# Four PSUM banks for transposes and four for products behind an out-projection

## The chip, the cores and the metric

The kernel runs on one core of a Trainium2 chip. The metric is the device time of one execution in microseconds, taken as the median of several runs; beside it there is one execution under the hardware profiler, whose page and trace are read here. TensorE is called PE (PEld for its weight loads), VectorE DVE, ScalarE ACT, GpSimdE POOL, and the queue that issues most loads SP.

## The reference

One layer of a hybrid encoder on 1024 tokens with 1024 channels, in float32:

```python
h = rms_norm(x, mix_pre_norm)
proj = h @ w_in                                   # 1024 x 2472
o_gdn = gated_deltanet_group(...)                 # chunkwise delta rule, 4 heads
o_mla = mla_group(...)                            # latent attention, 8 heads, block-causal
mixed = concatenate([o_gdn, o_mla], -1) @ w_out
x = x + rms_norm(mixed, mix_post_norm)
h = rms_norm(x, ffn_pre_norm)
f = square(relu(h @ w_up)) @ w_down               # 1024 -> 4096 -> 1024
x = x + rms_norm(f, ffn_post_norm)
```

Only the part from `w_out` to `w_up` bears on the change.

## The kernel before

Every float32 product is made of three passes in a reduced type: both operands are split into a high and a low half (`hi`, `lo`), and `mm3` (L206 to L209) multiplies hi x hi, lo x hi and hi x lo into one PSUM bank. ACT makes the high half by a cast, DVE the low half by a subtraction; both read the same source. One 128x512 product of three passes over four blocks of rows is thus 12 PE instructions.

The tokens are handled in eight blocks of 128 rows, t = 0 to 7. The end of the mixer and the start of the channel mixer go like this:

- `out_proj(t)` (L1236) adds the attention heads' part of the output projection to what is kept in `part[t]`, in two banks of tag `out` (for t from 2 on). It then normalises: the row sums of squares on ACT, a chain of small DVE instructions, and at L1256 the last reads of the two banks, by DVE. A residual addition and a second normalisation follow, and the result is written back to `part[t]`.
- `put(block, src, c)` (L1275) brings 128x512 of it to the layout that the next product needs: four PE transposes into one bank of tag `tr` (tile `ps_h2T`, L1279), then per pair of target tiles a cast by ACT (L1284) and a subtraction by DVE (L1285), which both read that bank. One such group is called a put here.
- `ffn_in(t)` (L1291) calls `put`. For blocks 0 to 3 it fills the tiles `B11` and `B21`. The up-projection works on 2x2 blocks with seven products in place of eight, for which blocks 4 to 7 are combined with blocks 0 to 3: for each of them five puts fill `T1`, `T2`, `T4`, `B22` and `T3`, with a DVE addition or subtraction of rows ahead of most. So there are 20 puts for blocks 4 to 7.
- `filler(p)` (L1357) does two of the products of every second weight pair ahead of time, since they need only `B11` and `B21`: 12 instructions against `B11` into a bank of tag `ps` (tile `ps_up`), a copy out of it by ACT (L1370) and to memory, 12 instructions against `B21` into the same bank, then relu and square by ACT (L1378, L1379) and a store (L1380). There are eight of them, 192 PE instructions. Their weights arrive by loads in the order of use (`load_chained`, L183), into buffers that become free when an earlier filler has been stored or when a row tile has been transposed.
- `up_pair(p)` (L1427) then does the rest of the up-projection pair by pair, beginning with `T1` times the pair's weight sums. `prepare(p)` (L1405) makes these sums (L1413, L1414) and splits them (L1336, L1337).

The text calls the fillers the first to the eighth, and the halves of one its B11 and its B21 half. The instructions are recorded by a tile layer that sets semaphores, hands out buffers and orders the instructions of each engine by a model of its own, so that the order in which an engine runs them is not the order of the lines. Each engine and the load queue run their own order strictly in sequence.

PSUM has eight banks of 128x512 float32 values. `psum_pool` gives them out by tag: it ends the pool before and opens a new one, in which each tag has so many banks, taken in turn; a tile in a new pool waits for the tiles that lay in its bank before.

```python
    def psum_pool(name, **bufs):                                   # L122
        ps_stack.close()
        pp[:] = [ps_stack.enter_context(tc.tile_pool(name=name, bufs=1, space=PSUM, reuse_waits="tile")), bufs]
...
    psum_pool("psC", out=4, tr=2, ps=2)                            # L1214
...
        ps = psum("ps_h2T", "tr")                                  # L1277, in put
        for j in range(4):
            transpose(ps[:, j * P : (j + 1) * P], src[:, j * P : (j + 1) * P], ident)
        n = 4 // len(block)
        for i, pair in enumerate(block):
            hi, lo = cut(pair, slice(None), slice(None), slice(c * P, (c + 1) * P))
            s = blocks3(ps[:, i * n * P : (i + 1) * n * P])
            nc.scalar.copy(hi, s)
            nc.vector.tensor_sub(lo, s, hi.bitcast(F32))
```

The stage's outer loop (L1477 to L1497) runs `out_proj` for all blocks, with `ffn_in` for blocks 0 to 3 two blocks behind and one filler's steps at the end; then `ffn_in` for blocks 4 to 7 with a step of a filler at each of its yields; then the rest of the fillers and the first `prepare`; and last `psum_pool("psD", ps=8)` for the up-projection.

Of the kernel before, what the change touches and what calls it, by code (L numbers as in the profile page):

```python
# [104 lines left out]
def build(tc, a, out):  # L105
# [16 lines left out]
# [3 lines that stand above are left out]
        for tag in bufs:  # L125
            psum2("order") if tag == "ps2" else psum("order", tag)
# [3 lines left out]
    def psum(name, tag="ps"):  # L130
        return pp[0].tile([P, HALF], F32, name=name, tag=tag, bufs=pp[1][tag])

    def psum2(name):
        return pp[0].tile([P, 2, HALF], F32, name=name, tag="ps2", bufs=pp[1]["ps2"])
# [1101 lines left out]
    def out_proj(t):  # L1236
        h = part[t]
        xt = gtile("xt")
        nc.sync.dma_start(xt, a["x"][t * P : (t + 1) * P, :])
        if t not in early:  # L1240
            ss1[t] = small([2], "ss1")
            banks = [psum("ps_out", "out") for n in range(2)]
            for n, ps in enumerate(banks):

                other = h[:, n * HALF : (n + 1) * HALF]
                nc.scalar.copy(ps, other)
                out_pairs(ps, t, n, range(NPAIR), onto=True)
                nc.scalar.activation(other, ps, AF.Square, accum_out=ss1[t][:, n : n + 1])
        else:
            banks = [h[:, :HALF], h[:, HALF:]]  # L1250
        ss = ss1[t]
        nc.vector.tensor_scalar(ss[:, 0:1], ss[:, 0:1], ss[:, 1:2], None, op0=ALU.add)
        r = rstd_of(ss[:, 0:1], D, "rpost")
        for n, ps in enumerate(banks):
            s = slice(n * HALF, (n + 1) * HALF)
            nc.vector.scalar_tensor_tensor(h[:, s], ps, r, gb[:, s], op0=ALU.mult, op1=ALU.mult)  # L1256
        nc.vector.tensor_add(xt, xt, h)
        nc.scalar.dma_start(d_x1[t], xt)
        ss2 = small([1], "ss2")
        nc.scalar.activation(h, xt, AF.Square, accum_out=ss2)  # L1260
        r2 = rstd_of(ss2, D, "rffn")
        nc.vector.scalar_tensor_tensor(h, xt, r2, gf, op0=ALU.mult, op1=ALU.mult)
# [28 lines left out]
    def ffn_in(t):  # L1291

        h = part[t]
        if t < 4:
            put(B11, h[:, first_half], t)
            put(B21, h[:, second_half], t)
            return
        if t == 4:
            later.update(T1=big("T1", bp, "b"), B22=big("B22", bp, "b"), T2=halves_of("T2", mtile))
        o, c = part[t - 4], t - 4  # L1300
        t2 = gtile("t2")[:, :HALF]
        nc.vector.tensor_sub(o[:, first_half], h[:, first_half], o[:, first_half])
        put(later["T1"], o[:, first_half], c)
        yield
        nc.vector.tensor_sub(t2, h[:, second_half], o[:, first_half])
        put(later["T2"], t2, c)
        yield
        nc.vector.tensor_sub(o[:, second_half], o[:, second_half], t2)
        if t == 4:
            later.update(T4=halves_of("T4", mtile), T3=halves_of("T3", gtile))  # L1310
        put(later["T4"], o[:, second_half], c)
        yield
        put(later["B22"], h[:, second_half], c)
        yield
        nc.vector.tensor_sub(h[:, first_half], h[:, second_half], h[:, first_half])
        put(later["T3"], h[:, first_half], c)
        part[t] = part[t - 4] = None
        yield
# [104 lines left out]
    def run(g):  # L1423
        if g is not None:
            next(g, None)
# [52 lines left out]
    for t in range(NT):  # L1478
        out_proj(t)
        if 2 <= t < 6:  # L1480
            for _ in ffn_in(t - 2):
                pass
        if t >= 6:
            run(fill)
            run(fill)
    for t in range(4, NT):
        for _ in ffn_in(t):
            run(fill)
# [237 lines left out]
```

## Time and profile before

| | |
|---|---|
| median of three runs | 1275.88 us (1275.73, 1275.88, 6953.69) |
| the profiled execution | 1274.2 us |
| its span, first to last instruction | 1272.5 us |
| TensorE busy | 1223.9 us, 96% of the span |
| VectorE, ScalarE, GpSimdE busy | 901.6, 656.4, 160.0 us |
| mean granted TensorE clock | 0.988 of full speed |
| moved by DMA | 205.72 MB, 162 GB/s |

The profile's page gives these sums. The stage of the change lies at about 600 to 700 us of the span, the up-projection behind it. In rows of the timeline, a line number names the line of the kernel, the arrow goes from what is read to what is written, and brackets give the idle time of the engine before the instruction with what ended it. The views by stretches give the busy time of each engine, then the granted clock (1.00 is full speed), the share of DMA engines in use and GB/s.

### The profile page before, as it was taken

How to read it: one execution, taken by the hardware profiler on the slowest of the kernel's cores; microseconds unless marked ns; L12 is line 12 of the kernel's file. 1: busy time of each engine (PE TensorE's matmuls, PEld its weight loads, DVE VectorE, ACT ScalarE, POOL GpSimd, SP SyncE). 2: the span in 40 equal slices, each digit the busy share in tenths (PEclk: the TensorE clock that was granted, in tenths of full speed). 3: DMA queues.
4: the chain of work that ended last, by engine and by line, in shares of the span. 5: the costliest groups of instructions: out<-in, count | busy, mean ns of one | idle time of the engine just before them, and what ended most of it. 6: DMA issues, size and time to landing. Idle time of an engine off the chain costs nothing.

```text
span 1272.5 us, 17691 instructions
## 1 busy us (share of the span) xinstructions
PE 1223.9 (96%) x6228; PEld 1035.0 (81%) x6228; DVE 901.6 (71%) x1779; ACT 656.4 (52%) x1201; POOL 160.0 (13%) x148
## 2 busy tenths in 40 slices
PE   7999999999889999999898999999999999999997
PEld 6978888899778878887686888888888888888885
DVE  7678879645556786686985677768666687775665
ACT  6467743325645786675665445445445443343341
POOL 1011001220044553430000000000000000010120
PEclk9999999999999999999998999999999999999998
DMA  5124534736342511123454355454449984547821
GB/s 234 34 75 146 190 120 174 232 79 182 97 145 87 162 50 31 42 67 150 148 186 161 124 181 210 165 198 174 174 157 388 400 323 153 193 159 237 282 89 66
DMA packets 111219, 205.72 MB, mean 162 GB/s; under 512 B 33558, under 2 KB 51990, under 8 KB 111131
## 3 DMA queue, kind: packets, MB, share of 16 engines
q1 hardware_dynamic: 93696, 171.90, 40.3%
q10 hardware_dynamic: 17434, 32.70, 6.9%
q8 instruction: 49, 0.80, 0.3%
q14 instruction: 40, 0.32, 0.1%
HBM read 143.07 MB, written 61.49 MB: 161 GB/s over the span
## 4 chain that ended last, share of the span: by engine, by line
PE 63%; DVE 3%; ACT 3%; DMA 2%; issue 1%; POOL 0%; SPq 0%; ACTq 0%; DVEq 0%; POOLq 0%
PE ps_up L208 8%; PE ps_up L209 8%; PE ps_up L207 8%; PE ps_dn L208 8%; PE ps_dn L209 8%; PE ps_dn L207 8%; PE ps_PT L1061 2%; PE ps_out L207 2%; PE ps_out L209 2%; PE ps_out L208 2%; PE ps_o L1080 1%; PE ps_sc L207 1%; PE ps_o L1079 1%; PE ps_sc L208 1%; PE ps_sc L209 1%
## 5 line engine op out<-in xcount | busy, mean ns | idle before, releaser
L1588 POOL TENSOR_TENSOR rows<-rows,gpost 128x512 f32<-128x512 f32 x12 | 20.1, 1703 | 617.8 <-ACT junk L1585 617.8
L209 PE MATMUL ps_proj<-hThi,wlo 128*128 128x512 f32 x192 | 75.1, 395 | 1.2 <-DVE wlo L199 1.2
L207 PE MATMUL ps_proj<-hThi,whi 128*128 128x512 f32 x192 | 76.0, 396 | 0.0
L208 PE MATMUL ps_proj<-hTlo,whi 128*128 128x512 f32 x192 | 76.0, 396 | 0.0
L1065 DVE TENSOR_TENSOR PTlo<-ps_PT,PThi 128x512 fp32r<-128x512 f32 (+2 forms) x96 | 52.0, 550 | 20.0 <-ACT PThi L1064 19.3
L1064 ACT CAST PThi<-ps_PT 128x512 fp32r<-128x512 f32 (+2 forms) x96 | 45.3, 480 | 30.1 <-PE ps_PT L1061 28.5
L1520 DVE TENSOR_TENSOR dlo<-draw,dhi 128x1024 fp32r<-128x1024 f32 x35 | 44.7, 1293 | 21.6 <-ACT dhi L1519 21.5
L208 PE MATMUL ps_dn<-dlo,dhi 128*128 128x512 f32 x144 | 56.0, 389 | 0.0
L209 PE MATMUL ps_dn<-dhi,dlo 128*128 128x512 f32 x144 | 56.0, 389 | 0.0
L1519 ACT CAST dhi<-draw 128x1024 fp32r<-128x1024 f32 x35 | 36.2, 1050 | 37.9 <-issue 13.8
L207 PE MATMUL ps_dn<-dhi 128*128 128x512 f32 x144 | 55.0, 389 | 0.0
L1035 ACT ACTIVATE Pt<-ps_sc,nm 128x896 f32<-128x896 f32 (+3 forms) x64 | 47.9, 749 | 11.8 <-DVE nm L1033 7.6
L1336 ACT CAST whi<-raw 128x1024 fp32r<-128x1024 f32 (+1 forms) x29 | 25.9, 904 | 51.4 <-PE ps_up L208 49.7
L1061 PE MATMUL ps_PT<-ident,Pt 128*128 128x128 f32 x288 | 46.4, 275 | 3.2 <-DVE PTlo L1065 1.9
L1033 DVE TENSOR_REDUCE nm<-ps_sc 128x1 f32<-128x896 f32 (+3 forms) x64 | 47.8, 750 | 1.2
L199 DVE TENSOR_TENSOR wlo<-raw,whi 128x1024 fp32r<-128x1024 f32 (+1 forms) x27 | 33.8, 1254 | 18.1 <-ACT whi L198 15.5
L1040 POOL TENSOR_TENSOR Pt<-Pt,rs 128x128 f32<-128x128 f32 (+4 forms) x40 | 35.4, 884 | 88.5 <-DVE rs L1038 64.4
L209 PEld LDWEIGHTS ps_proj<-hThi,wlo 128*128 128x128 f32 x192 | 36.1, 188 | 9.2 <-DVE wlo L199 1.7
L1079 PE MATMUL ps_o<-PThi,V 128*128 128x256 f32 (+1 forms) x160 | 40.5, 276 | 2.9 <-DVE o L1086 1.2
L208 PEld LDWEIGHTS ps_proj<-hTlo,whi 128*128 128x128 f32 x192 | 36.1, 188 | 7.4 <-issue 0.5
L207 PEld LDWEIGHTS ps_proj<-hThi,whi 128*128 128x128 f32 x192 | 36.1, 188 | 7.4 <-issue 0.5
L1061 PEld LDWEIGHTS ps_PT<-ident,Pt 128*128 128x128 f32 x288 | 34.0, 140 | 8.6 <-issue 2.5
(596 smaller groups left out, 3978.0 us busy)
## 6 DMA issues: line engine op xcount, KB each, us to landing
draw<-in_w_down_dram SPq DMA_DIRECT2D x47, 512.0 KB
draw<-d_act SPq DMA_DIRECT2D x41, 512.0 KB
raw<-in_w_up_dram SPq DMA_DIRECT2D x40, 512.0 KB
raw<-in_w_down_dram SPq DMA_DIRECT2D x17, 512.0 KB
raw<-in_w_qkvg_dram SPq DMA_DIRECT2D x16, 512.0 KB
d_act<-c SPq DMA_DIRECT2D x16, 512.0 KB
d_act<-s SPq DMA_DIRECT2D x16, 512.0 KB
raw<-d_act SPq DMA_DIRECT2D x15, 512.0 KB
```

Of the source, the lines that this page charges most:

```text
L207: mm(ps, lhs[0], rhs[0], start=start, stop=False, **kw)
L208: mm(ps, lhs[0], rhs[1], start=False, stop=False, **kw)
L209: mm(ps, lhs[1], rhs[0], start=False, stop=stop, **kw)
L1033: nc.vector.tensor_reduce(nm, ps[:, :npc, :w], axis=AX.XY, op=ALU.max, negate=True)
L1035: nc.scalar.activation(Pt[:, :n].rearrange("p (i w) -> p i w", i=npc), ps[:, :npc, :w], AF.Exp, bias=nm, scale=1.0, accum_out=sm)
L1040: nc.gpsimd.tensor_tensor(Pt[:, :n], Pt[:, :n], rs.to_broadcast([P, n]), op=ALU.mult)
L1061: transpose(ps[:, j * P : (j + 1) * P], Pt[:, b * P : (b + 1) * P], ident)
L1064: nc.scalar.copy(hi[:, :n, cs], ps3)
L1065: nc.vector.tensor_sub(lo[:, :n, cs], ps3, hi[:, :n, cs].bitcast(F32))
L1079: mm(ps[:, cs], V[h][:, b], hi[:, cs], start=(b == 0), stop=False)
L1519: nc.scalar.copy(hi, raw)
L1520: nc.vector.tensor_tensor(lo, raw, hi.bitcast(F32), op=ALU.subtract)
```

## The change

One line is added, ahead of the loop over blocks 4 to 7:

```diff
         if t >= 6:
             run(fill)
             run(fill)
+    psum_pool("psT", tr=4, ps=4)
     for t in range(4, NT):
         for _ in ffn_in(t):
             run(fill)
```

Until now the pool of L1214 held for the whole stage: four banks for `out_proj`, two for puts, two for products. Now its eight banks are given out anew once the last `out_proj` has been recorded: four for puts, which lie where the four of `out` were, and four for products, which lie where `tr` and `ps` were. Since the first filler is recorded before this line, it still uses a bank of the old pool, and all 20 puts of blocks 4 to 7 and the other seven fillers use the new one. As the banks enter into what the tile layer orders, the order of the instructions changes on PE, DVE and ACT from here to the first product with `T1`. Up to here and, but for buffer numbers and a few single rows, from there on it is as it was.

On PE, the first filler ends its B11 half like this in the order before (`part_4795` is the row tile of block 0, here being put into T1 with block 4 subtracted):

```order
L207 MATMUL ps_up<-B11hi,whi 128x512
L208 MATMUL ps_up<-B11lo,whi 128x512
L209 MATMUL ps_up<-B11hi,wlo 128x512
L1279 MATMUL ps_h2T<-ident,part_4795 128x128 x4
L208 MATMUL ps_up<-B11lo,whi 128x512
L209 MATMUL ps_up<-B11hi,wlo 128x512
L207 MATMUL ps_up<-B11hi,whi 128x512
```

And like this in the order of the change:

```order
L207 MATMUL ps_up<-B11hi,whi 128x512
L208 MATMUL ps_up<-B11lo,whi 128x512
L209 MATMUL ps_up<-B11hi,wlo 128x512
L207 MATMUL ps_up<-B21hi,whi 128x512
L208 MATMUL ps_up<-B21lo,whi 128x512
L209 MATMUL ps_up<-B21hi,wlo 128x512
L207 MATMUL ps_up<-B21hi,whi 128x512
```

Block 4's first put and the second filler's B11 half stood between the two halves of the first filler; now the B21 half follows directly, and that put comes after its twelve instructions.

On PE, the last puts stand like this in the order before, at the end of the eighth filler (`part_5806` and `part_5975` are the rows of blocks 6 and 7, `part_5308` those of block 3, `t_7272` a difference of both):

```order
L1279 MATMUL ps_h2T<-ident,part_5806 128x128 x4
L208 MATMUL ps_up<-B21lo,first_hi 128x512
L209 MATMUL ps_up<-B21hi,first_lo 128x512
L1279 MATMUL ps_h2T<-ident,part_5806 128x128 x4
L1279 MATMUL ps_h2T<-ident,part_5308 128x128 x4
L1279 MATMUL ps_h2T<-ident,t_7272 128x128 x4
L1279 MATMUL ps_h2T<-ident,part_5308 128x128 x4
L1279 MATMUL ps_h2T<-ident,part_5975 128x128 x8
L207 MATMUL ps_up<-T1hi,wv_hi 128x512
```

And like this in the order of the change, in the B21 half of the sixth filler:

```order
L1279 MATMUL ps_h2T<-ident,t_7278 128x128 x4
L1279 MATMUL ps_h2T<-ident,part_5308 128x128 x4
L207 MATMUL ps_up<-B21hi,whi 128x512
L208 MATMUL ps_up<-B21lo,whi 128x512
L1279 MATMUL ps_h2T<-ident,part_5975 128x128 x4
L209 MATMUL ps_up<-B21hi,wlo 128x512
L207 MATMUL ps_up<-B21hi,whi 128x512
L208 MATMUL ps_up<-B21lo,whi 128x512
L209 MATMUL ps_up<-B21hi,wlo 128x512
L1279 MATMUL ps_h2T<-ident,part_5975 128x128 x4
L207 MATMUL ps_up<-B21hi,whi 128x512
```

The six puts at the end stood behind all fillers, with two products ahead of the last five; now products stand between them, and from the last put to the first product with `T1` there are 49 products of fillers.

On ACT, the casts of weights stand like this in the order before, in the middle of the fillers (`whi<-raw_7300` and `first_hi<-raw` are the seventh and eighth filler's weights, and the casts from `ps_h2T` belong to the puts of blocks 4 and 5):

```order
L1336 CAST whi<-raw_7153 128x1024
L1371 DMA d_p_102<-raw 128x512
L1336 CAST whi<-raw 128x1024
L1284 CAST T3hi_7036<-ps_h2T 128x2x128
L1284 CAST T1hi<-ps_h2T 128x4x128
L1378 ACTIVATE raw<-ps_up 128x512
L1379 ACTIVATE raw<-raw 128x512
L1284 CAST T3hi_7038<-ps_h2T 128x2x128
L1380 DMA d_act_109<-raw 128x512
L1336 CAST whi<-raw_7300 128x1024
L1378 ACTIVATE raw<-ps_up 128x512
L1336 CAST first_hi<-raw 128x1024
```

And like this in the order of the change (`raw_7306` is the seventh filler's weights there, `d_act_108` the store of the second filler):

```order
L1336 CAST whi<-raw_7306 128x1024
L1379 ACTIVATE raw<-raw 128x512
L1371 DMA d_p_101<-raw 128x512
L1370 COPY raw<-ps_up 128x512
L1380 DMA d_act_108<-raw 128x512
L1371 DMA d_p_102<-raw 128x512
L1284 CAST T2hi_6993<-ps_h2T 128x2x128
L1284 CAST T2hi_6995<-ps_h2T 128x2x128
L1284 CAST T4hi_7038<-ps_h2T 128x2x128
L1284 CAST T4hi_7040<-ps_h2T 128x2x128
L1336 CAST first_hi<-raw 128x1024
```

The weights' casts have moved ahead in relation to the fillers' results: the seventh filler's cast now stands before the second filler's square and store, and the eighth filler's cast only one store and two puts behind.

## The prediction

> **What bounds the kernel now.** The page comes first: how much of the span is TensorE, and how it runs where nothing disturbs it.
>
> ```profile
> span 1272.5 us, 17691 instructions
> PE 1223.9 (96%) x6228; PEld 1035.0 (81%) x6228; DVE 901.6 (71%) x1779; ACT 656.4 (52%) x1201; POOL 160.0 (13%) x148
> 800.00:1000.00 200.00, 199.95 (x881) 165.01 (x880) 136.25 (x175) 92.03 (x114) 0.00 (x0) 1.00 0.62 228
> ```
>
> TensorE is busy for 96% of the span. The third row is a stretch of the view by stretches (length, then busy time and count of PE, PEld, DVE, ACT and POOL, granted clock, DMA share, GB/s): 200 us of the up-projection, 881 products of 512 columns without a gap, so **0.227 us per product**. A change of banks removes no work; it can only win TensorE's idle time and its time at a low clock. So the second view looks for both around the edited line, which stands between the out-projection and the last blocks' transposes.
>
> ```profile
> 684.00:688.00 4.00, 2.51 (x17) 1.70 (x16) 2.56 (x5) 3.17 (x7) 0.00 (x0) 1.00 0.41 158
> 688.00:692.00 4.00, 1.48 (x8) 0.87 (x6) 4.00 (x8) 3.40 (x7) 0.00 (x0) 0.63 0.39 131
> 692.00:696.00 4.00, 2.17 (x8) 1.91 (x9) 4.00 (x7) 1.82 (x4) 0.00 (x0) 0.50 0.60 195
> 696.00:700.00 4.00, 4.00 (x12) 3.19 (x11) 4.00 (x8) 1.65 (x3) 0.00 (x0) 0.59 0.19 72
> ```
>
> Here is the hole: 16 us with PE busy for 10.2, and the clock at 0.50 to 0.63 for most of it. The timeline of PE alone says what it waits for (start, length, instruction, idle time before it and its releaser).
>
> ```profile
> 684.36 0.60 PE L1279 MATMUL ps_h2T<-ident,part 128*128 128x128 f32 x4
> 685.46 0.66 PE L1279 MATMUL ps_h2T<-ident,part 128*128 128x128 f32 x4 [0.50 <-DVE B22lo L1285]
> 686.91 0.63 PE L1279 MATMUL ps_h2T<-ident,t 128*128 128x128 f32 x4 [0.79 <-DVE T3lo L1285]
> 687.73 0.66 PE L1279 MATMUL ps_h2T<-ident,part 128*128 128x128 f32 x4 [0.20 <-DVE T1lo L1285]
> 690.62 1.09 PE L1279 MATMUL ps_h2T<-ident,part 128*128 128x128 f32 x4 [2.23 <-DVE T2lo L1285]
> 693.83 1.08 PE L1279 MATMUL ps_h2T<-ident,part 128*128 128x128 f32 x4 [2.12 <-DVE T4lo L1285]
> 694.56 0.78 PE L207 MATMUL ps_up<-T1hi,wv_hi 128*128 128x512 f32 x1
> ...
> 699.58 0.40 PE L207 MATMUL ps_up<-T2hi,wv_hi 128*128 128x512 f32 x1
> ```
>
> Six puts (four transposes each, into one bank) stand at the end with no products left between them. Each is released by the DVE subtraction that empties the bank of the put two before it: two banks, so each put waits for ACT's cast and DVE's subtraction. DVE is 4.00 of 4.00 busy from 688 on, since the first pair's weight sums stand in its queue between those subtractions. The first product runs at a halved clock, and full pace is back at 699.58.
>
> **The change, part by part.** First the price of a put, from the stretch before the hole, where puts stand between products:
>
> ```profile
> 637.81:684.13 46.32, 46.32 (x231) 38.37 (x230) 29.21 (x55) 25.86 (x53) 0.00 (x0) 1.00 0.55 192
> 637.81:684.13 46.32, 7.61 (x52) 6.40 (x53) 10.01 (x21) 8.68 (x22) 1.00 0.55 192
> ```
>
> The second row is the same stretch for ps_h2T alone: 52 transposes, 13 puts. Of the other 179 matmuls one began before it; (46.32 - 178 x 0.227) / 13 = 0.455 us per put.
>
> *The hole goes (-9.8).* From 684.36 to 699.58 are 15.2 us. Their work at full pace is 6 x 0.455 + 12 x 0.227 = 5.45 us, so 9.8 us are lost. In the changed order all puts stand among fillers, 49 filler products follow the last one, and a put waits for the fourth put before it. What must keep up is DVE:
>
> ```profile
> 636.00:700.00 64.00, 58.16 (x275) 47.37 (x275) 45.58 (x82) 36.65 (x72) 0.00 (x0) 0.91 0.49 173
> ```
>
> Its 45.6 us of this stretch must fit into 64 - 7.3 = 56.7 us: 80%, so the cover holds on average.
>
> *A wait for the out-projection's banks (0).* The new transposes' banks lie where `out` lay, so block 4's T1 and T2 wait for the last readers of out_proj(6)'s banks, T4 and B22 for those of out_proj(7)'s.
>
> ```profile
> 640.83 1.40 DVE L1256 SCALAR_TENSOR_TENSOR part<-ps_out,rpost,gpost 128x512 f32<-128x512 f32 x2
> ```
>
> These end at 642.23, and DVE's new order puts them ahead of T1lo, so no later. PE comes to T4 at 645.6 (below). The 3.4 us between are the cover; beyond it every us costs one, since all of PE's queue stands behind that put.
>
> *The first filler now stands alone (+0.5).* Before, T1's put and the second filler's products lay between its B11 and B21 halves. Now its B21 half follows at once, into the same bank, which ACT must copy first.
>
> ```profile
> 636.10 0.63 PE L209 MATMUL ps_up<-B11hi,wlo 128*128 128x512 f32 x1
> 636.53 1.05 PE L1279 MATMUL ps_h2T<-ident,part 128*128 128x128 f32 x4
> 637.24 0.74 PE L208 MATMUL ps_up<-B11lo,whi 128*128 128x512 f32 x1
> 637.81 0.40 PE L209 MATMUL ps_up<-B11hi,wlo 128*128 128x512 f32 x1
> 636.82 0.58 ACT L1370 COPY raw<-ps_up 128x512 f32<-128x512 f32 x1 [4.31 <-PE ps_up L209]
> ```
>
> The twelfth product starts at 636.10, the copy ends at 637.40, PE resumes at about 637.45. From 636.53 to 637.81 it does 0.84 of a product (0.36 / 0.427) instead of a put and a whole one: behind by 0.455 + 0.04 = 0.5 us. The queue behind this product holds everything.
>
> *The clock comes back later (+1.6).* These are stretches of 3.41 us between the edges of the granted clock:
>
> ```profile
> 627.57:630.98 3.41, 0.87 (x5) 0.33 (x3) 2.47 (x8) 2.75 (x6) 0.00 (x0) 1.00 0.08 32
> 630.98:634.39 3.41, 2.86 (x7) 2.15 (x7) 3.41 (x11) 0.99 (x2) 0.00 (x0) 0.50 0.00 0
> 634.39:637.81 3.42, 3.42 (x11) 2.73 (x10) 3.42 (x7) 0.77 (x2) 0.00 (x0) 0.50 0.00 0
> 637.81:641.22 3.41, 3.41 (x16) 2.82 (x15) 3.41 (x8) 2.14 (x4) 0.00 (x0) 1.00 0.58 231
> 695.83:699.25 3.42, 3.42 (x9) 2.65 (x9) 3.42 (x8) 1.42 (x2) 0.00 (x0) 0.50 0.25 96
> ```
>
> PE waits for B11 from 627.85 to 630.38, and from 630.98 the clock is 0.50. A stretch with 2.86 of 3.41 busy is followed by another at 0.50; full ones (634.39, 695.83) are followed by 1.00. With the new wait the stretch 634.39 to 637.81 holds 636.73 - 634.39 + 0.36 = 2.7 us, less than 2.86. So I take one more stretch at half pace: 3.41 x (1 - 0.227 / 0.427) = 1.6 us, with 0.427 the step from 636.10 to 636.53. The bounds are 0 and two stretches, 3.2; I take one, by the row of 2.86. The Trainium skill, "TensorE: Matmul & The Clock Gate", section "What's actually happening", says that the clock is judged in free-running windows of 3413 ns and released after one busy window. The trace agrees in the grid: from 630.98 to 637.81 are two windows, from there to 699.25 eighteen. By that rule with only a full window counting as busy the sum gets this 1.6, with a four-fifths one 0.
>
> *Loads and ACT's queue (+0.4).* The last fillers' weights are cast ahead of block 5's and 6's evacuations in ACT's new order, and DVE's subtraction `first_lo` stands ahead of those too. The load of the last filler's weights waits for the store of the second filler's result.
>
> ```profile
> 655.76 1.67 SPq L183 DMA_DIRECT2D raw<-in_w_up_dram  x1
> 661.93 1.06 ACT L1336 CAST first_hi<-raw 128x1024 fp32r<-128x1024 f32 x1 [1.05 <-DMA raw<-in_w_up_dram]
> 663.02 1.22 DVE L1337 TENSOR_TENSOR first_lo<-raw,first_hi 128x1024 fp32r<-128x1024 f32 x1
> 686.00 0.33 ACTq L1380 DMA_DIRECT2D d_act<-raw  x1
> 688.05 5.65 SPq L183 DMA_DIRECT2D raw<-in_w_up_dram  x3
> ```
>
> A load takes up to 6.2 us (655.76 to 661.93), a store frees its buffer after about 2 (686.00 to 688.05). By the cadence above (637.45, plus 0.227 a product, 0.455 a put, and 1.8 for the half clock since 637.45) PE comes to T4's put of block 4 at 645.6 (24 products, 2 puts), ends the second filler at 652.4 (46, 6), comes to block 6's T4 at 668.5 (105, 12) and to the first T1 product at 689.2 (180, 20). The second filler's square follows on ACT by 655 to 658, its store at 656.4 to 658.3, the load 2 us later, the data at 662.5 to 666.5, and after cast, `first_lo` and B22lo (1.06 + 1.22 + 0.7) block 5's bank is free at 665.5 to 669.5, where 668.5 is needed; the next bank is needed 0.45 later and comes 0.4 + 0.7 later. So 0 to 1.6 us; I take 0.4, as only the late end of each estimate misses.
>
> *The sum:* -9.8 + 0.5 + 1.6 + 0.4 = -7.3 us. The profiled execution took 1274.2 us, its span of 1272.5 and 1.7 around it: 1266.9. The median of the runs is 1275.88, 1.7 above that execution; on its scale 1268.6, which I give. All else in the built program keeps its order but for single rows, and the up-projection stays without gaps, as in 800 to 1000.
>
> **The rivals.**
>
> *The clock returns at 637.81 all the same.* For it: 2.7 busy is near 2.86, and another execution's grid lies elsewhere. Against: the row of 2.86. The sum is 1.6 better: 1267.
>
> *The first pair's weights become the wait.* Before, they were ready just ahead of their use:
>
> ```profile
> 677.74 1.09 SPq L183 DMA_DIRECT2D raw<-in_w_up_dram  x2
> 687.59 0.68 DVE L1413 TENSOR_TENSOR sums<-raw 128x512 f32<-128x512 f32 x1
> 690.99 1.22 DVE L1337 TENSOR_TENSOR wv_lo<-sums,wv_hi 128x1024 fp32r<-128x1024 f32 x1
> ```
>
> If `wv_lo` still ended at 692.2 (690.99 + 1.22), the third T1 product would wait for it from 689.7: 2.5 us, and by the row of 627.57 such an idle window can halve the clock again for one or two windows, 1.6 to 3.2. That gives 1271 to 1274.5. For it: its loads still wait for the fillers' stores and stand last in SP's queue. Against: they wait for the third and fourth filler's stores alone, and by the cadence those end at 661.5 and 665.6; with 4 us for ACT and the store the loads start 7 to 12 us before 677.74.
>
> *Slower than before: the last filler's load starves the banks.* One mechanism: PE's queue stands at block 6's puts behind ACT's cast of weights that have not landed. Each us after about 665.5 costs one, and 1.6 to 3.2 once a window is half idle; the gain of 7.3 is eaten from a landing at about 670.5 on, 8 us later than the early estimate. It would give 1276 to 1282. For it: ACT and DVE are strictly in order there. Against: the longest load in the rows above took 6.2 us, and the DMA share is 0.55.
>
> *It does not do what it says:* the puts move, but the waits move with them to other bank reuses inside the fillers, and DVE's total sets the pace after all: 1275 to 1277. Against: the 80% of DVE.
>
> **How the numbers follow.** Forecast 0.54 (1265.5 to 1271), clock back early 0.20 (1264 to 1268), weights 0.15, slower 0.07, nothing gained 0.04. A range from 1263.5 to 1274.5 leaves out the last two and some edge of the others, less than 2 in 10, and holds the bounds of the clock (0 to 3.2) and of the loads (0 to 1.6). A measurement of this kernel can tell about 2% from no change, 25.5 us. No case but a pile-up of several stalls or an unseen gain reaches that: faster 0.01, within 0.98, slower 0.01.
>
> **What would show it.** In the changed profile: no idle row at L1279 after the fillers, and T1's first product at about 689 with the clock at 1.00; a wait of about 0.9 us of L207 (ps_up from B21) for ACT's copy near 637; the clock at 0.50 until about 641; PE in 700 to 1000 as full as now. The forecast is wrong if L1279 waits for B22lo or T1lo near 668, if L209 on `wv_lo` waits at 689, or if the half clock comes again between 641 and 690.

## The result, and the profile after

The changed kernel took **1267.7 us** (median of six runs, 1266.31 to 1268.59), the kernel before 1275.89 in the same set (six runs from 1272.38 on; one of them, 6953.69, stands far outside and is left out of the comparison). The ratio is 0.9937, with a 95% interval of 0.9921 to 0.9952. The forecast was 1268.6 within 1263.5 to 1274.5. Run again beside the experiments, in another set, the ratio was 0.9959 (0.9939 to 0.9978), with 1268.13 against 1274.15.

The page of the changed kernel:

```profile
span 1265.9 us, 17687 instructions
PE 1220.9 (96%) x6228; PEld 1032.8 (82%) x6228; DVE 898.9 (71%) x1779; ACT 655.2 (52%) x1201; POOL 160.1 (13%) x148
```

The work is the same, the span is 6.6 us shorter. What PE waits for from 600 to 705 us (engine, line, releaser; then us in total, times, longest):

```profile
PE ps_up L207 <- ACT B11hi L1284: 2.6, 1, 2.6
PE ps_out L207 <- ACT ps_out L1246: 2.3, 3, 1.4
PE ps_up L207 <- ACT raw L1370: 2.0, 2, 1.3
PE ps_up L208 <- DVE B11lo L1285: 0.8, 1, 0.8
```

No wait of L1279 is left: the six puts that stood at the end of the fillers now run among them without idle time. Two waits for ACT's copy (L1370) are new. The timeline of PE has both, and the two ends of the stretch in which the change acts:

```profile
625.75 0.40 PE L209 MATMUL ps_out<-whi,mixlo 128*128 128x512 f32 x1
636.67 0.80 PE L207 MATMUL ps_up<-B21hi,whi 128*128 128x512 f32 x1 [0.73 <-ACT raw L1370]
...
680.32 0.39 PE L209 MATMUL ps_up<-B11hi,wlo 128*128 128x512 f32 x1
...
683.04 0.39 PE L209 MATMUL ps_up<-B11hi,first_lo 128*128 128x512 f32 x1
684.73 0.50 PE L207 MATMUL ps_up<-B21hi,whi 128*128 128x512 f32 x1 [1.30 <-ACT raw L1370]
690.31 0.39 PE L207 MATMUL ps_up<-T1hi,wv_hi 128*128 128x512 f32 x1
693.03 0.39 PE L207 MATMUL ps_up<-T2hi,wv_hi 128*128 128x512 f32 x1
```

**The stretch** is taken from the start of the out-projection's last product to the start of the first product with T2. Here it is 693.03 - 625.75 = 67.28 us. In the kernel before, that last product began at

```profile
626.57 0.40 PE L209 MATMUL ps_out<-whi,mixlo 128*128 128x512 f32 x1
```

and with T2 at 699.58 it was 73.01. So the stretch is 5.7 us shorter; behind it lie 572.9 us in both (1265.9 - 693.03 and 1272.5 - 699.58). The other 0.8 us of the two spans' difference come ahead of the change (625.75 against 626.57).

The granted clock around the first filler, in stretches between its edges (length, busy time of PE, PEld, DVE, ACT, POOL, then clock, DMA share, GB/s; such a stretch of 3.41 us is called a window from here on):

```profile
626.79:630.20 3.41, 0.73 (x4) 0.19 (x1) 2.43 (x8) 2.76 (x6) 0.00 (x0) 1.00 0.09 36
630.20:633.61 3.41, 2.72 (x6) 2.15 (x7) 3.41 (x11) 0.98 (x2) 0.00 (x0) 0.50 0.00 0
633.61:637.03 3.42, 2.69 (x7) 1.67 (x6) 3.42 (x7) 0.58 (x1) 0.00 (x0) 0.50 0.00 0
637.03:640.44 3.41, 3.41 (x9) 2.64 (x9) 3.41 (x7) 1.15 (x2) 0.00 (x0) 0.50 0.58 231
```

The half clock lasts three windows, where it lasted two: the new stall of 0.73 us falls into the second. The new stall at 684.73 is read from DVE's and ACT's timelines:

```profile
678.83 0.69 DVE L1413 TENSOR_TENSOR sums<-raw 128x512 f32<-128x512 f32 x1 [4.25 <-DMA raw<-in_w_up_dram]
679.43 0.42 DVE L1285 TENSOR_TENSOR T2lo<-ps_h2T,T2hi 128x256 fp32r<-128x256 f32 x1
679.88 0.37 ACT L1284 CAST T2hi<-ps_h2T 128x256 fp32r<-128x256 f32 x1 [4.01 <-DVE T2lo L1285]
684.07 0.61 ACT L1370 COPY raw<-ps_up 128x512 f32<-128x512 f32 x1
```

DVE stands idle for 4.25 us before the first pair's weight sum, whose load has not landed. Behind it waits a subtraction of a put, behind that ACT's next cast, and behind ACT's casts the copy of the seventh filler's B11 half, whose last product began at 680.32. PE does the eighth filler's B11 half meanwhile (to 683.04), then comes to the seventh's B21 half, which goes into the bank still to be copied, and waits.

### The profile page after: what moved, and what is told of

Its sections match the earlier page's. It is cut to its first block, busy times and chain, and to the rows that moved or that the text cites. A ratio compares the mean times of both kernels' runs of the same rounds, so it can differ in the third digit from the quotient of the medians.

```text
span 1265.9 us, 17687 instructions
## 1 busy us (share of the span) xinstructions
PE 1220.9 (96%) x6228; PEld 1032.8 (82%) x6228; DVE 898.9 (71%) x1779; ACT 655.2 (52%) x1201; POOL 160.1 (13%) x148
## 4 chain that ended last, share of the span: by engine, by line
PE 61%; ACT 4%; DVE 4%; DMA 2%; issue 1%; POOL 0%; ACTq 0%; SPq 0%; DVEq 0%; POOLq 0%
PE ps_dn L208 8%; PE ps_dn L209 8%; PE ps_dn L207 8%; PE ps_up L207 7%; PE ps_up L208 7%; PE ps_up L209 7%; PE ps_PT L1061 2%; PE ps_out L207 2%; PE ps_out L209 2%; PE ps_out L208 2%; PE ps_o L1080 1%; PE ps_sc L207 1%; PE ps_o L1079 1%; PE ps_sc L208 1%; PE ps_sc L209 1%
```

## The experiments

Whole runs of one kernel differ by 2 to 11 us within a set (the changed one: 1266.31 to 1268.59 in one set, 1265.6 to 1272.1 in another; the one before: 1269.77 to 1280.38), so each experiment has its ratio and beside it the stretch of its profiled execution, as defined above, with what lies behind it. The sets differ in level, so medians are compared within a set only:

| kernel | ratio to before (95%) | stretch, us | from T2's first product to the end, us |
|---|---|---|---|
| before | 1 | 73.01 | 572.9 |
| changed | 0.9937 (0.9921 to 0.9952) | 67.28 | 572.9 |
| changed, again | 0.9959 (0.9939 to 0.9978) | 66.69 | 573.2 |
| tr=2, ps=2 | 1.0065 (1.005 to 1.008) | 79.52 | 572.9 |
| tr=4, ps=2 | 0.9967 (0.9954 to 0.998) | 65.76 | 572.6 |
| tr=2, ps=4 | 1.0078 (1.006 to 1.0096) | 77.71 | 572.7 |
| tr=3, ps=5 | 1.0015 (1.0 to 1.0029) | 73.06 | 572.9 |
| two products in the first filler's stall | 0.9944 (0.9932 to 0.9956) | 64.66 | 572.7 |
| ten products ahead of the first filler | 0.9945 (0.9924 to 0.9965) | 64.19 | 572.6 |
| sums behind the last put | 0.9947 (0.9928 to 0.9966) | 65.44 | 572.6 |
| both of these | 0.9962 (0.9948 to 0.9976) | 63.36 | 572.8 |
| another ring of load buffers | 1.0006 (0.9989 to 1.0024) | 63.81 | 580.1 |
| two buffers exchanged | 0.9943 (0.9928 to 0.9958) | 65.58 | 572.5 |
| exchanged, and ten products | 0.9953 (0.9939 to 0.9968) | 62.44 | 573.5 |

The theory: the transposes' banks carry the gain, and it is smaller than the hole because of the clock's third window and two stalls at ACT's copy. The rivals: the new order alone carries it, or the products' banks do; and the half clock has nothing to do with the stall.

### Which banks carry the gain

```diff
-    psum_pool("psT", tr=4, ps=4)
+    psum_pool("psT", tr=2, ps=2)
```

> The pool is opened anew at the same line, but with two banks for transposes and two for products, as before the change; four banks stay unused. Theory (the number of transposes' banks carries the gain): the last six puts stand behind the fillers again and wait as before, so the hole of 9.8 us stays, and the first filler stands alone as in the changed kernel, so its stall (0.5) and the third window at half clock (1.6) are paid without the gain: 1276 to 1279, at or above the kernel before (1275.9). Rival (any second pool at this place, by the new order that it brings, gives the gain): 1267 to 1270.

```diff
-    psum_pool("psT", tr=4, ps=4)
+    psum_pool("psT", tr=4, ps=2)
```

> Only the transposes get banks: four for them, two for products. Theory: the whole gain is here, since a filler's product waits for the bank of two products back, which a square or a copy freed long ago: 1266.5 to 1269.5, within 1 us of the changed kernel (1267.7). Rival (the product banks carry it): 1275 to 1279, with PE waiting for the bank of the filler before.

```diff
-    psum_pool("psT", tr=4, ps=4)
+    psum_pool("psT", tr=2, ps=4)
```

> Only the products get banks: two for transposes, four for products. Theory: the six puts at the end wait for DVE's subtractions again: 1275 to 1279. Rival (product banks): 1267 to 1270.

Measured were 1280.0, 1267.97 and 1282.62 us beside 1272.15 of the kernel before in that set. So only the version with four banks for transposes is faster; with two it is slower than before, whether products have two banks or four. (With tr=2, ps=4 the stretch explains 4.7 of the 10.5 us; in its profiled execution the rest lies ahead of the stretch, and why is open.) The timeline of PE with tr=2, ps=2, at the end of the fillers, shows where most of the 7.9 us go that it loses, more than the 0 to 3 of the theory:

```profile
688.99 0.66 PE L1279 MATMUL ps_h2T<-ident,t 128*128 128x128 f32 x4 [1.81 <-DVE T1lo L1285]
692.73 1.09 PE L1279 MATMUL ps_h2T<-ident,part 128*128 128x128 f32 x4 [2.64 <-DVE T2lo L1285]
695.93 1.09 PE L1279 MATMUL ps_h2T<-ident,part 128*128 128x128 f32 x4 [2.12 <-DVE T4lo L1285]
700.73 0.76 PE L207 MATMUL ps_up<-T1hi,wv_hi 128*128 128x512 f32 x1 [3.72 <-DVE T3lo L1285]
```

These waits sum to 10.3 us, where the six puts and the first product with T1 waited for 0.50 + 0.79 + 0.20 + 2.23 + 2.12 = 5.8 before. With the stall of the first filler (its price in the forecast: 0.5) and the third window (1.6) that makes 4.5 + 2.1 = 6.6, and the stretch is 6.5 longer. So with two banks the puts wait as before (6.6 us against 5.8), and most of the loss is side costs of opening the pool anew.

The largest of these, the 3.72 us, is one that the theory had not. The product with T1 reads nothing of T3, so what it waits for must be its bank: in the up-projection's pool it lies where a bank of the transposes lay, and the last put's subtraction empties that late. In the kernel before, T1's first product ran at 694.56, long before that subtraction:

```profile
698.07 0.42 DVE L1285 TENSOR_TENSOR T3lo<-ps_h2T,T3hi 128x256 fp32r<-128x256 f32 x1
```

This is read from the rows and the program; no run tests it by moving the banks alone.

With tr=4, ps=2 PE has one wait that the changed kernel has not (`PE ps_h2T L1279 <- DVE t L1305: 1.8, 1, 1.8` in its list of waits), but neither the stall of the seventh filler (1.46 by starts, see below) nor the third window (1.6). 1.8 - 1.46 - 1.6 = -1.3; its stretch is 1.5 and 0.9 shorter than the changed kernel's two. That the third window is missing can't be put down to the banks: the first filler's stall is the changed kernel's, and only the clock's edges lie elsewhere (see the account of the prediction). So by the stretch nothing of the gain hangs on the products' banks. The whole runs show it less sharply: 4.2 us below the kernel before here, where the changed kernel has 8.2 and 6.0 in two other sets.

```diff
-    psum_pool("psT", tr=4, ps=4)
+    psum_pool("psT", tr=3, ps=5)
```

> Three banks for transposes, five for products. Theory (what counts is that DVE's evacuation of a put is off PE's path, and puts that come three in a row need as many banks): all puts stay among the products but the last, which stands ahead of T1; the hole stays away, 0 to 2 us above the changed kernel, ratio 0.995 to 0.998. Rival (four are needed): waits of 2 us at L1279 come back, ratio 0.999 to 1.002.

1274.08 us, and the stretch is as long as before: the expectation failed. The rival's ratio is right, its reason isn't, since L1279 waits nowhere. PE's timeline and DVE's:

```profile
694.62 0.76 PE L207 MATMUL ps_up<-T1hi,wv_hi 128*128 128x512 f32 x1 [5.50 <-DVE T3lo L1285]
```

```profile
688.55 1.23 DVE L1337 TENSOR_TENSOR wlo<-raw,whi 128x1024 fp32r<-128x1024 f32 x1
690.62 1.81 DVE L1337 TENSOR_TENSOR wlo<-raw,whi 128x512 fp32r<-128x512 f32 x2
694.05 0.41 DVE L1285 TENSOR_TENSOR T3lo<-ps_h2T,T3hi 128x256 fp32r<-128x256 f32 x1
```

With three banks the last put stands right ahead of T1's products, and its evacuation stands in DVE's queue behind the first pair's weights. T1's product again waits for a bank, as with tr=2, ps=2: PE waits 5.5 us, and the clock drops for two windows. A fourth bank lets the last put run 49 products earlier. Whether three banks would do if they lay where the up-projection does not begin, no run shows; the puts themselves had enough of them.

### The clock's third window

```diff
         nc.scalar.copy(x[:, first_half], ps)
         nc.scalar.dma_start(d_p1[p // 2], x[:, first_half])
+        if p == 0:
+            idle = psum("ps_up")
+            for _ in range(2):
+                after(mm(idle, w[0][:, :P], w[0][:, :HALF], start=True, stop=True).ins, m, "behind B11's last product")
         yield
```

(`m` is B11's last product.)

> The changed kernel with two more products (their result is not used, they go to a bank of their own) between the first filler's B11 half and its B21 half, where PE waits 0.9 us for ACT's copy at half clock: 2 x 0.427 = 0.85 us. No other instruction moves. Theory (the stall empties a part of the second 3.41-us window and so holds the clock down for a third one): the second window after the drop is now full, the clock is back after two windows (6.83 us instead of 10.24), and 1.6 us are won: 1266.1. Rival (the time at half clock does not hang on this stall): the clock is back after three windows all the same, 1267.7, or up to 0.1 above.

PE's timeline and the windows of this kernel:

```profile
636.81 1.05 PE L1375 MATMUL ps_up<-whi 128*128 128x512 f32 x2
637.74 0.50 PE L207 MATMUL ps_up<-B21hi,whi 128*128 128x512 f32 x1
```

```profile
627.48:630.90 3.42, 1.04 (x9) 0.76 (x7) 2.64 (x7) 2.39 (x5) 0.00 (x0) 1.00 0.14 56
630.90:634.31 3.41, 2.75 (x7) 1.88 (x7) 3.41 (x13) 1.36 (x3) 0.00 (x0) 0.50 0.00 0
634.31:637.72 3.41, 3.41 (x9) 2.24 (x7) 3.41 (x5) 0.59 (x1) 0.00 (x0) 0.50 0.00 0
637.72:641.14 3.42, 3.42 (x18) 2.87 (x18) 3.42 (x9) 1.51 (x3) 0.00 (x0) 1.00 0.57 230
```

With the second window full the clock is back after two, as the theory says, though two products more are done. The stretch is 2.0 to 2.6 us shorter (1.6 expected; another 0.5 is the seventh filler's stall, 0.79 us in this execution and not 1.30). By whole runs the gain isn't shown: its ratio, 0.9944, lies between the changed kernel's two.

```diff
         ps = psum("ps_up")
+        if p == 0:
+            for _ in range(10):
+                mm(ps, w[0][:, :P], w[0][:, :HALF], start=True, stop=True)
         for k in range(4):
             mm3(ps, k_slice(w, 0, k), moving(B11, k), k == 0, k == 3)
```

> The changed kernel itself, beside the others and the kernel before on this chip. Expected is the ratio of the first set, 0.9937 (0.992 to 0.995), whatever the level of the chip.

> The changed kernel with ten more products (their result is not used) just ahead of the first filler's, where PE waits 2.6 us for ACT's cast of B11: 10 x 0.227 = 2.3 us, so nothing real starts later. Theory (the clock falls because that wait empties a 3.41-us window): the clock stays at 1.00 from 627 to 641, the first filler's 24 products win up to 3 x 1.6 = 4.8 us, of which the first put of block 4 gives back about 1.6, since its operand is ready at 638.1 by DVE's full queue and PE would be there at 636.5: 3.2 below the changed kernel, 1.6 to 4.8. Rival (the clock falls for another reason, or the wait of 0.8 us for DVE's subtraction of B11 is enough for it): no gain, 0 to 0.3 us.

The changed kernel came to 1268.13 us here, the one with ten products ahead of its first filler to 1265.52, 2.6 less; the stretch is 2.5 to 3.1 shorter. Its windows, and four rows of its list of waits (L1373 is the copy, L1370 in the other kernels; the wait of 0.8 us for `B11lo` stayed):

```profile
627.10:630.52 3.42, 3.20 (x18) 2.42 (x16) 2.48 (x5) 2.31 (x5) 0.00 (x0) 1.00 0.14 54
630.52:633.93 3.41, 2.63 (x11) 1.92 (x12) 3.41 (x14) 1.44 (x3) 0.00 (x0) 1.00 0.00 0
633.93:637.35 3.42, 2.69 (x12) 1.90 (x11) 3.42 (x5) 0.59 (x1) 0.00 (x0) 1.00 0.20 77
```

```profile
PE ps_up L207 <- ACT raw L1373: 1.3, 2, 0.7
PE ps_h2T L1279 <- DVE T1lo L1285: 0.8, 1, 0.8
PE ps_h2T L1279 <- DVE T2lo L1285: 0.5, 1, 0.5
PE ps_up L207 <- ACT B11hi L1284: 0.2, 1, 0.2
```

The clock stays at 1.00 through the first filler. So the wait for B11 is what halves it, and 4.8 us of three windows could be won; some of it comes back as waits for puts (1.3 us), since DVE has not become faster. By the stretch most of the expectation holds; the intervals of the two ratios overlap.

### The seventh filler's stall

```diff
-            nc.vector.tensor_sub(lo, s, hi.bitcast(F32))
+            last_put[:] = [nc.vector.tensor_sub(lo, s, hi.bitcast(F32)).ins]
...
-        nc.vector.tensor_add(s[:, first_half], r2[:, first_half], r2[:, second_half])
+        add = nc.vector.tensor_add(s[:, first_half], r2[:, first_half], r2[:, second_half]).ins
+        if p == 0:
+            after(add, last_put[0], "sums behind the last put")
```

> The changed kernel with one order more: DVE's first sum for the first pair's weights stands behind its last subtraction of a put. Theory (the seventh filler's B21 half waits for ACT's copy, since ACT's queue waits there for a T2lo that stands behind that sum's load on DVE): the stall of 1.3 us near 684 goes, 1.3 below the changed kernel. Rival (the sums are then late for T1's products at 689): a wait for wv_lo takes its place, 0 to 2 us above.

1265.91 us against 1268.13, with intervals that overlap; the stretch is 1.3 and 1.8 shorter than in the two executions of the changed kernel. PE has no wait for ACT's copy (L1370) but the first filler's, and none for `wv_lo`. On DVE the sum now follows the last put at once (this edit shifts the line numbers by two):

```profile
678.88 0.42 DVE L1287 TENSOR_TENSOR T3lo<-ps_h2T,T3hi 128x256 fp32r<-128x256 f32 x1 [0.44 <-ACT T3hi L1286]
679.22 0.68 DVE L1415 TENSOR_TENSOR sums<-raw 128x512 f32<-128x512 f32 x1
682.23 1.22 DVE L1339 TENSOR_TENSOR wv_lo<-sums,wv_hi 128x1024 fp32r<-128x1024 f32 x1 [0.40 <-ACT wv_hi L1338]
```

It begins at 679.22, where it began at 678.83 in the changed kernel: moving it behind seven subtractions cost it 0.4 us, since it had only waited for its load. `wv_lo` ends at 683.45, over 5 us ahead of its use.

The two edits together (the ten products and this order):

> The changed kernel with both edits: the ten products whose result is not used ahead of the first filler, and DVE's sums for the first pair behind the last put. Theory (two separate losses, the clock and the seventh filler's stall): their gains add up, 2.6 + 1.3 to 2.2: 4 to 5 us below the changed kernel, a ratio to the kernel before of 0.992 to 0.993. Rival (both took the same slack, so the second brings nothing): as one of them alone, 0.9945.

In the stretch the gains add up for the most part (63.36, 3.3 to 3.9 less than the changed kernel, where the two alone had 3.8 to 4.9 together), but the median, 1268.39, doesn't show it: the expected ratio was missed. The profiled execution lost time ahead of the stretch: DVE waited for a tile of x in the out-projection, and PE for what follows from it.

```profile
598.49 1.23 DVE L1257 TENSOR_TENSOR xt<-xt,part 128x1024 f32<-128x1024 f32 x1 [2.17 <-DMA xt<-in_x_dram]
```

```profile
604.19 0.50 PE L207 MATMUL ps_out<-whi,first_hi 128*128 128x512 f32 x1 [3.47 <-ACT ps_out L1246]
```

The changed kernel's first profile has 1.40 us at that place, and the last product of the out-projection comes at 625.75 there, at 631.65 here. Of these 5.9 us, 2.2 were there before the wait (the product that waits for the same copy one step earlier began at 589.52, in the changed kernel at 587.35), 2.1 are the wait, and 1.6 a window at half clock right behind it. Whether this explains all eleven runs is open, as one of them was profiled.

### The wait for B11 itself

ACT's cast of B11 stands behind its cast of the third filler's weights, whose load waits for a buffer that a tile of x holds. The buffers are taken in a fixed turn, called the ring here.

```diff
-        r = gtile("raw") if raws[0] % 4 == 3 else raw_tile()
+        r = gtile("raw") if raws[0] % 4 == 0 else raw_tile()
```

> The changed kernel with another choice of buffers for the weights' loads: every fourth one goes to a buffer of the x tiles, and it is now the fourth, not the third. The third filler's load then waits for no x tile, its cast no longer stands in ACT's queue as a wait ahead of B11's. Theory (B11's cast is late because ACT waits 1.6 us for that load): the first product of the fillers comes 1.9 us sooner, its hole shrinks from 2.6 to 0.7 us, so the window is 80% busy and the clock mostly stays: 4 to 6 us below the changed kernel; with the clock falling all the same 1.9 below. Rival (DVE, full from 630 to 641, sets the pace behind it): the time comes back as a wait of the first puts, 0 to 1 below.

The fillers did begin sooner, and the stretch is 2.9 to 3.5 us shorter; yet the kernel was 5.5 us slower than the changed one. The loss lies 330 us later, at the start of the down-projection:

```profile
957.81 2.08 PE L207 MATMUL ps_dn<-first_hi,whi 128*128 128x512 f32 x4 [4.95 <-ACT first_hi L1520]
```

The same ring of buffers serves those loads, and they now land too late; two windows at half clock follow. Neither theory had that. So only the two buffers at stake were exchanged, with all later ones as they were:

```diff
-        r = gtile("raw") if raws[0] % 4 == 3 else raw_tile()
+        r = gtile("raw") if raws[0] == 4 or (raws[0] > 4 and raws[0] % 4 == 3) else raw_tile()
```

> The changed kernel with the third and the fourth filler's buffers for their weights exchanged (the third gets a plain one, the fourth the one of the x tiles), and all later loads as they were. Theory (the other ring lost 7 us at the start of the down-projection alone, where its loads met the buffers in another order): the early start of the fillers stays, first product 2.5 us sooner, the stretch to T1 1.5 us shorter, the down-projection starts without a wait: 4 us below the changed kernel, ratio 0.992 to 0.994. Rival (the loss hangs on the early end of the fillers, or on the third load itself): the wait of 5 us near 953 stays, ratio 0.999 to 1.001.

> The exchange of the two buffers together with the ten products ahead of the first filler (their result is not used). With the exchange PE waits 0.8 us for B11's cast and then 2.3 us for its subtraction; ten products of 0.227 end before that subtraction does. Theory: nothing real is delayed and the clock stays at 1.00, two windows of 1.6 us less: 2 to 3 us below the exchange alone. Rival (the clock is not what bounds the first filler here, DVE is): 0 to 1 below.

With the exchange the wait of 5 us is gone (572.5 us behind T2), which shows it was the ring's; the ratio is 0.9943, just outside what the theory gave, and the stretch 1.1 to 1.7 shorter than the changed kernel's. PE's timeline tells why it isn't more: a wait went over to DVE's half of B11.

```profile
628.89 0.50 PE L207 MATMUL ps_up<-B11hi,whi 128*128 128x512 f32 x1 [0.83 <-ACT B11hi L1284]
631.68 0.79 PE L208 MATMUL ps_up<-B11lo,whi 128*128 128x512 f32 x1 [2.28 <-DVE B11lo L1285]
```

The clock still falls for three windows (631.02 to 641.26). With ten products ahead of it as well, it stays at 1.00 and the stretch is another 3.1 us shorter, about what they won before, and the shortest of all. But the median is 1267.0: of its profiled execution 0.7 us went into waits for `wv_hi` and `wv_lo` and 0.6 into one at the down-projection, and a tile of x was late as above (PE waited 4.0 us for it). For the other runs this is open. So several versions have a shorter stretch than the changed kernel, and the lowest single run was 1263.59 us, with the exchange; none is shown to beat it in whole runs.

## Why the prediction was right

- **The hole (-9.8).** Right. No put waits at the end, and where the number of `tr` banks is two again, the puts' waits are back (6.6 us).
- **The wait for the out-projection's banks (0).** Right: no row of L1279 is idle near block 4's puts.
- **The first filler alone (+0.5).** Right as far as it is seen: the stall is there, 0.73 us where about 0.9 was forecast, in the place of a put and a product's worth of work. The 0.5 itself was not measured alone.
- **The clock (+1.6).** Right in size, one window more in both executions, and that the stall causes it is shown by the two products that took it away. The reason given, too little busy time in the window, is not the whole of it, so the number owes something to where the edges fell. The rival, a return at 637.81, came true in another kernel: with tr=4, ps=2 the second window is as empty and the clock was back all the same.

```profile
633.77:637.18 3.41, 2.69 (x7) 1.58 (x5) 3.41 (x5) 0.59 (x1) 0.00 (x0) 0.50 0.00 0
637.18:640.59 3.41, 3.40 (x17) 2.85 (x18) 3.41 (x9) 1.49 (x3) 0.00 (x0) 1.00 0.58 231
```

- **Loads and ACT's queue (+0.4).** Right in the range, wrong in the place. The eighth filler's weights were cast at 664.30 and the bank that hung on them cost PE nothing: 0. But the first pair's weights, a rival with 0.15, showed up in part. They were on time for T1, where the rival put its wait. They were late for DVE's queue, and through DVE and ACT held up the seventh filler's copy: from 683.04 to 684.73 are 1.69 us, 1.46 more than a product takes. This term of the sum was missing. The rival had been held small because 4 us were to lie between the fourth filler's end and the load that follows its store. That filler's last product began at 664.69, early enough, but ACT's queue stood behind the eighth filler's cast, the store was issued at 669.71, and the load that waited for a store started at 674.75, nearly 10 us after that product.

```profile
664.30 1.05 ACT L1336 CAST first_hi<-raw 128x1024 fp32r<-128x1024 f32 x1 [3.08 <-DMA raw<-in_w_up_dram]
669.71 0.35 ACTq L1380 DMA_DIRECT2D d_act<-raw  x1
674.75 0.33 SPq L183 DMA_DIRECT2D raw<-in_w_up_dram  x1
```

With what was measured in place of the last term, the sum is -9.8 + 0.5 + 1.6 + 0 + 1.5 = -6.2 us; the two executions show -5.7 and -6.3 in the stretch, where -7.3 were forecast. The medians differ by 8.2 in the first set and by 6.0 in the second, so the forecast lies between. That it came within 0.9 us of the first set's median is partly luck: the stretch won less than forecast, and the rest of the 8.2 is not in it. Scatter ahead of the stretch is the likely source, but this isn't shown. T1's first product came at 690.31, where 689.2 were forecast, with the first filler 0.78 us earlier than in the execution of before: 1.9 late, of which 1.46 is that stall.

The Trainium skill, "TensorE: Matmul & The Clock Gate", section "What's actually happening", has the full clock come back after at least one busy window and the windows run free of the kernel. The trace agrees in both (edges 3.41 us apart, windows that are full at half clock followed by 1.00 in every execution), but a window of 2.69 us of 3.41 was followed by 0.50 in the changed kernel and by 1.00 with tr=4, ps=2, so busy time alone doesn't decide it.

## What to carry to other kernels

When an evacuation runs on two engines and each of their queues holds other work, count the banks by how late the evacuation may come, not by how long it takes: with two banks the puts waited here, with three the first product behind them did, in the changed kernel with four neither. When a pool is opened anew, ask also which bank its first tile takes over, and who empties that bank last. Removing such a hole moves all that was hidden behind it: look in each in-order queue for the one instruction that waits for a load, and for who stands behind it, to the third engine. And before a load buffer is given to someone else, follow its ring to the end of the kernel.

## What the runs showed of the hardware

- What a window does to the clock depends on more than its busy time. At full clock, windows with 2.63 and 2.69 us busy of 3.41 were followed by full clock (ten products ahead); at half clock, windows of 2.69 were followed by half clock in the changed kernel and by full clock with tr=4, ps=2. In that second case PE's idle time reached to the window's end (it resumed at 637.19, the edge is at 637.18), in the first it ended 0.36 us before. Of eighteen windows at half clock with 2.6 to 2.9 us busy in all the executions profiled, the two whose idle time reached to the edge (the other is in the kernel with another ring of buffers) were followed by full clock, the other sixteen by half clock. Why that should matter was not settled.
- Work that serves nothing can be cheaper than idling: ten products of 0.227 us in a wait of 2.6 us were followed by a stretch 2.5 to 3.1 us shorter.
- DVE waited 2.17 us for the load of a tile of x in one execution and not at all in another. PE's wait behind it and a window at half clock made 3.7 of the 5.9 us by which the ends of the out-projection lie apart (631.65 and 625.75). That is over half of what this change is worth, so that a change of this size is read from a stretch of the trace better than from whole runs.
